# A hybrid decoder layer: the second half's attention projections take their token tiles from a pool that opens after the mixers

## The chip, the cores and the metric

One Trainium2 chip; the program runs on one of its cores. The metric is the device time of one execution in microseconds (us). TensorE is called PE, VectorE DVE, ScalarE ACT, GpSimd POOL and SyncE SP; PEld is PE's weight load. SP issues most of the DMAs, ACT issues some.

## What is computed

One decoder layer over 2048 tokens of width 1024. A combined projection feeds three groups of heads, whose outputs are joined and projected back; then a feed-forward part follows. The reference, cut to that:

```python
h = RMSNorm(x)
p = h @ w_in                      # columns split among three groups
A = mLSTM(p[...])                 # 4 heads, width 256, chunkwise
B = RWKV7(p[...])                 # 4 heads, width 256, delta-rule state
C = diff_attention(p[...])        # 4 heads, width 512, causal, blocks of 128 queries
x = x + concat(A, B, C) @ w_out
x = x + relu(RMSNorm(x) @ w_ff_up)**2 @ w_ff_down
return RMSNorm(x)
```

All of it is float32 in and out. The kernel multiplies in a split form: each operand is a high and a low part, and a product is three matmuls (`mm3`, L182 to L184: high by high, high by low, low by high).

## The kernel before

**Halves and columns.** The tokens stand as four column blocks of 512, two to a half. `Proj` holds the normalised tokens of one half as 16 tiles of 128x512 in a high and a low part (`hhi`, `hlo`). `start(half)` makes them: for each of the 16 tiles it loads 256 KB (`raw`, a tile `xk` from the pool `xp`, three buffers), multiplies it by the norm's factors on DVE (L324), writes the high part on ACT (L174) and the low part on DVE or POOL by turns (L175). Since `hhi` and `hlo` have one buffer for each column block, a second `start` overwrites them.

**Projections.** `feat` keeps weights stationary and runs 24 matmuls of 512 columns into one of two PSUM buffers `pd`; `token` keeps tokens stationary and runs 24 matmuls of 256 columns. `cols_a` makes the attention's columns of one half: four `feat` units (keys into `akh`, `akl`, queries into `aqh`, `aql`) of four `pd` tiles each, 384 matmuls of 512, and two `token` units (values into `av`) of eight tiles each, 384 matmuls of 256. All results go to DRAM.

**Mixers.** Sixteen iterations of `Rwkv` (prepare, scores, invert, chain, post: L505 to L777) and of `Mlstm` (up to L939) work on 128 tokens each, software-pipelined over five iterations: when iteration 15 is prepared, 12 is in its chain. The chain is a recurrence over the state `rST` with two steps to an iteration. Each step goes from PE (L717, L720) to a DVE copy `rZ`, to PE (L725), to copies `rUE` and `rUO`, to PE (L730, L733), and to DVE again (L735, L740). `post` ends with four POOL operations, transposes on PE (L772), copies on ACT (L774) and stores to `mixT` (L777).

**Order.** A scheduler places the instructions of each engine in one list, ahead of time, by priorities: the mixers have numbers from 100000 on, the projections 1000000, so that projections stand as filler between the mixers' operations wherever their data and buffers allow it. Pools are opened and closed like a stack, from a left and from a right side; a tile that takes the space of a closed pool waits for the last users of that space. The mixers' pools `rp` and `mp` lie on the right and close with `mctx.close()`; the pools of `Attention` (L942) open in that space, so its work can't begin before the mixers' end either. `Attention.run(c)` works on one column block: scores (L1004, L1005), their eviction with a maximum (L1008), exponentials (L1016), transposes (L1029), copies `PT` (L1031) and products with the values (L1034). `attn.run(0)` and `attn.run(1)` need only the first half's columns, `attn.run(2)` and `attn.run(3)` need both. Then comes `Tail`: four column blocks, each with an out-projection from `mixT`, a norm and the feed-forward matmuls. It is filler behind the attention.

In the built list of before the second half's projections stand among the last mixer iterations; the values' last part stands beside the first attention block.

Of the kernel before, what the change touches and what calls it, by code (L numbers as in the profile page):

```python
# [10 lines left out]
F32 = mybir.dt.float32  # L11
# [9 lines left out]
P = 128  # L21
# [4 lines left out]
T = 512  # L26
# [14 lines left out]
def load(nc, i, out, in_):  # L41
    (nc.sync if i % 2 == 0 else nc.scalar).dma_start(out, in_)
# [6 lines left out]
class Lane:  # L49


    def __init__(s, tc, p):
        s.tc, s.p = tc, p
# [94 lines left out]
def norm(tc, e, sp, raw, pp, ptag, src, gofs, emit, w=T):  # L148

    nc = tc.nc  # L150
    n = w // P
    acc = sp.tile([P, T], F32, name="nacc", tag="nacc", bufs=1)[:, :w]
    for k in range(KT):
        if k == 0:
            nc.scalar.activation(acc, src[k], AF.Square)
        else:
            sq = raw()[:, :w]
            nc.scalar.activation(sq, src[k], AF.Square)
            nc.vector.tensor_tensor(acc, acc, sq, ALU.add)
    ps = pp.tile([P, T], F32, name="nps", tag=ptag)  # L160
    for tt in range(n):
        nc.tensor.matmul(ps[:, tt:tt + 1], acc[:, tt * P:(tt + 1) * P], e.ones[:, 0:1], start=True, stop=True)
    sm = sp.tile([P, 3, 4], F32, name="nsm", tag="nsm", bufs=2)[:, :, :n]
    nc.vector.tensor_scalar(sm[:, 0], ps[:, 0:n], 1.0 / D, NORM_EPS, ALU.mult, ALU.add)
    rsqrt(nc, e, sm[:, 1], sm[:, 0], sm[:, 2])
    ps = pp.tile([P, T], F32, name="nps", tag=ptag)[:, :w]
    bcast_rows(nc, e, raw()[:, :w], ps, sm[:, 1])
    nc.scalar.copy(acc, ps)
    for k in range(KT):
        emit(k, src[k], e.vf[:, gofs + k:gofs + k + 1], acc)  # L170
# [48 lines left out]
class Proj:  # L219


    def __init__(s, ctx, tc, e, xt, pools):
        s.tc, s.e, s.xt = tc, e, xt
        s.hhi, s.hlo, s.rst, s.rcol = {}, {}, {}, {}
        s.last = e.cp.tile([P, 5], F32, name="last")
        tc.nc.gpsimd.memset(s.last, 0.0)

        s.qlast = e.cp.tile([P, 4, 3], F32, name="qlast")
        tc.nc.gpsimd.memset(s.qlast, 0.0)
        s.ep = ctx.enter_context(tc.tile_pool(name="ep", bufs=2))  # L230
        s.evp = (s.ep, 3)
        s.hp = ctx.enter_context(tc.tile_pool(name="hp", bufs=1))
        s.w = Weights(tc, e, ctx.enter_context(tc.tile_pool(name="wp1", bufs=2)), 5, 528)
        s.xp = ctx.enter_context(tc.tile_pool(name="xp", bufs=2))
        s.pd = ctx.enter_context(tc.tile_pool(name="pd", bufs=2, space=PSUM))

        d, a, m, i, c, l = (s.pd, "pd"), *[(pools[k], k) for k in ("pa", "pm", "pi", "pc", "pl")]
        s.pn, s.more = (l, i), ((d, d, m, m), (a, c, d, d))

    def raw(s, half, c, k):  # L240
        x = s.xp.tile([P, T], F32, name="xk", tag="xk", bufs=3)
        load(s.tc.nc, k, x, s.xt[half * 2 + c, k])
        return x

# [937 lines left out]
def tile_hybrid_layer(ctx: ExitStack, tc: tile.TileContext, xt, wi, wg, wm, wo, wu, wd, vf, vg, lw, hb, tb, lq, cm, out, dbg=None, upto=9):  # L1182
# [23 lines left out]
    e.state = State(tc, keep)  # L1206
    NG = HALF // RC
    mctx = ExitStack()
    lctx, actx = ExitStack(), ExitStack()
    with tc.using_default_side("right"):  # L1210
        pa = mctx.enter_context(tc.tile_pool(name="pa", bufs=1, space=PSUM))
        pm = mctx.enter_context(tc.tile_pool(name="pm", bufs=2, space=PSUM))
# [3 lines left out]
    pr = Proj(lctx, tc, e, xt, dict(pa=pa, pm=pm, pi=pi, pc=pc, pl=pl))  # L1216
# [46 lines left out]
    mctx.close()  # L1263
    with tc.using_default_side("right"):
        attn = Attention(actx, tc, e)
    for c in range(2):
        attn.run(c)
    pr.start(1)
    pr.cols_a(wi)
    lctx.close()  # L1270
    for c in range(2, 4):
        attn.run(c)
# [105 lines left out]
```

## Time and profile before

| | us |
|---|---|
| median of 3 runs | 3096.33 (3092.64 to 3100.31) |
| the profiled execution | 3105.86 |
| its span, from the first to the last instruction | 3104.0 |
| PE busy | 2976.4 |
| DVE busy | 1759.6 |
| ACT busy | 1219.4 |
| POOL busy | 1108.4 |

Times in the trace count from the span's start. A matmul's end is modelled, so that consecutive matmuls overlap in the rows; their pace is the distance of their starts. The granted clock is a share of the full 2.4 GHz; half of it is the other level, so a mean between 0.5 and 1 in a window says which part of it ran at 1.2 GHz.

### The profile page before, as it was taken

The page shows a single profiled execution, that of the slowest core. Times are in us where ns is not written, and L with a number is a line of the kernel's source. Part 1 is how long each engine was busy: PE and PEld are TensorE (multiplying, and loading weights), DVE is VectorE, ACT ScalarE, POOL GpSimd, SP SyncE. Part 2 cuts the span into 40 slices and gives each one's busy share as a digit, 9 for nine tenths or more (in the row PEclk, how much of TensorE's full clock was granted, in tenths as well). Part 3 has the DMA queues.
Part 4 walks back from the last instruction along what each step waited for, and adds up shares of the span by engine and source line. Part 5 has one row for each costly group of instructions (what it writes and reads, how often), then busy time and mean ns, then how long its engine had stood idle before and what let it go on. Part 6 is the DMA issues. An engine that isn't in the chain of part 4 may idle for free.

```text
span 3104.0 us, 47480 instructions
## 1 busy us (share of the span) xinstructions
PE 2976.4 (96%) x17232; PEld 2447.8 (79%) x17232; DVE 1759.6 (57%) x4087; ACT 1219.4 (39%) x2421; POOL 1108.4 (36%) x1063
## 2 busy tenths in 40 slices
PE   8999999899989979999999999999999999999997
PEld 6887877777867867888888878888787888888885
DVE  6486788967884356556455665554365333333335
ACT  5342333423332445454545454444344222222223
POOL 4443344534443213433334433433454222222213
PEclk9999999999999979999999999999999999999998
DMA  5434332544343553444445444342442211111111
GB/s 177 142 108 122 85 93 67 149 118 117 91 122 111 164 144 109 117 123 110 108 110 152 111 132 103 91 120 75 128 143 79 69 51 52 41 48 50 52 42 65
DMA packets 284484, 317.38 MB, mean 102 GB/s; under 512 B 99253, under 2 KB 160982, under 8 KB 284250
## 3 DMA queue, kind: packets, MB, share of 16 engines
q1 hardware_dynamic: 203050, 213.02, 24.4%
q10 hardware_dynamic: 81200, 101.34, 11.3%
q8 instruction: 136, 2.23, 0.3%
q14 instruction: 98, 0.80, 0.1%
HBM read 256.82 MB, written 57.43 MB: 101 GB/s over the span
## 4 chain that ended last, share of the span: by engine, by line
PE 67%; DVE 7%; DMA 4%; ACT 1%; issue 1%; POOL 1%; SPq 0%; ACTq 0%; DVEq 0%; POOLq 0%
PE pd L182 11%; PE pd L184 11%; PE pd L183 11%; PE py L182 7%; PE py L183 7%; PE py L184 7%; PE pO L1034 4%; PE pS L1004 2%; PE pS L1005 2%; PE pT L1029 2%; DMA Qd<-aql 1%; PE pi L677 1%; DMA traw<-mixT 0%; DVE E L1008 0%; DVE E L1023 0%
## 5 line engine op out<-in xcount | busy, mean ns | idle before, releaser
L175 POOL TENSOR_TENSOR wlo<-wraw,whi 128x512 fp32r<-128x512 f32 (+2 forms) x560 | 763.1, 1375 | 1293.4 <-ACT whi L174 796.6
L174 ACT ACTIVATE whi<-wraw 128x512 fp32r<-128x512 f32 (+2 forms) x560 | 347.4, 626 | 676.6 <-PE py L183 392.8
L1154 DVE TENSOR_TENSOR x<-py,x 128x512 f32<-128x512 f32 x512 | 350.7, 689 | 458.6 <-PE py L184 456.2
L182 PE MATMUL pd<-hh,whi 128*128 128x512 f32 x1280 | 503.2, 396 | 9.3 <-ACT hh L174 9.2
L183 PE MATMUL pd<-hl,whi 128*128 128x512 f32 x1280 | 504.4, 395 | 0.4 <-DVE hl L175 0.4
L184 PE MATMUL pd<-hh,wlo 128*128 128x512 f32 x1280 | 501.9, 395 | 0.0
L182 PE MATMUL py<-ah,whi 128*128 128x512 f32 x1024 | 404.8, 398 | 1.5 <-ACT whi L174 1.3
L183 PE MATMUL py<-al,whi 128*128 128x512 f32 x1024 | 400.8, 394 | 0.6 <-DVE al L175 0.6
L184 PE MATMUL py<-ah,wlo 128*128 128x512 f32 x1024 | 399.4, 394 | 0.2 <-POOL wlo L175 0.2
L182 PEld LDWEIGHTS pd<-hh,whi 128*128 128x128 f32 x1280 | 241.0, 189 | 62.0 <-ACT hh L174 10.5
L183 PEld LDWEIGHTS pd<-hl,whi 128*128 128x128 f32 x1280 | 241.8, 189 | 53.2 <-DVE hl L175 1.1
L184 PEld LDWEIGHTS pd<-hh,wlo 128*128 128x128 f32 x1280 | 241.9, 189 | 52.1 <-issue 0.2
L1008 DVE TENSOR_SCALAR_CACHE_REDUCE E<-pS 128x512 f32<-128x512 f32 (+4 forms) x320 | 185.4, 606 | 128.3 <-PE pS L1005 86.0
L175 DVE TENSOR_TENSOR al<-traw,ah 128x512 fp32r<-128x512 f32 x128 | 112.2, 878 | 222.8 <-ACT ah L174 222.2
L182 PE MATMUL pd<-hhi,whi 128*128 128x512 f32 x544 | 225.1, 416 | 10.8 <-ACT hhi L279 8.0
L182 PEld LDWEIGHTS py<-ah,whi 128*128 128x128 f32 x1024 | 192.6, 188 | 44.6 <-ACT whi L174 1.7
L184 PEld LDWEIGHTS py<-ah,wlo 128*128 128x128 f32 x1024 | 192.5, 188 | 43.7 <-POOL wlo L175 0.6
L183 PEld LDWEIGHTS py<-al,whi 128*128 128x128 f32 x1024 | 192.7, 188 | 42.5 <-DVE al L175 0.8
L183 PE MATMUL pd<-hlo,whi 128*128 128x512 f32 x544 | 224.1, 414 | 0.0
L184 PE MATMUL pd<-hhi,wlo 128*128 128x512 f32 x544 | 223.5, 413 | 0.4 <-POOL wlo L175 0.4
L182 PE MATMUL pd<-whi,hhi 128*128 128x256 f32 (+1 forms) x640 | 190.0, 297 | 4.8 <-ACT ev L352 2.8
L183 PE MATMUL pd<-wlo,hhi 128*128 128x256 f32 (+1 forms) x640 | 190.3, 297 | 0.0
(367 smaller groups left out, 5189.6 us busy)
## 6 DMA issues: line engine op xcount, KB each, us to landing
wraw<-in_wu ACTq DMA_DIRECT2D x96, 256.0 KB, 3.1
wraw<-in_wu SPq DMA_DIRECT2D x96, 256.0 KB, 3.1
wraw<-in_wd ACTq DMA_DIRECT2D x96, 256.0 KB, 3.0
wraw<-in_wd SPq DMA_DIRECT2D x96, 256.0 KB, 3.0
wraw<-in_wi ACTq DMA_DIRECT2D x48, 256.0 KB, 3.3
wraw<-in_wi SPq DMA_DIRECT2D x48, 256.0 KB, 3.3
xk<-in_xt ACTq DMA_DIRECT2D x32, 256.0 KB, 3.7
xk<-in_xt SPq DMA_DIRECT2D x32, 256.0 KB, 3.2
```

The lines of the kernel that those rows point to most:

```text
L174: nc.scalar.activation(hi, src, AF.Copy)
L175: lo_eng.tensor_tensor(lo, src, hi.bitcast(F32), ALU.subtract)
L182: nc.tensor.matmul(out, sh, mh, start=(i == 0), stop=False)
L183: nc.tensor.matmul(out, sh, ml, start=False, stop=False)
L184: nc.tensor.matmul(out, sl, mh, start=False, stop=(i == n - 1))
L677: PE.matmul(q[HS[h2], pcx * 64:(pcx + 1) * 64], lhsT[pcx][h2], rhs[pcx][h2], start=True, stop=True)
L1004: PE.matmul(s_[:, :k1 - k0], Q[c][0][:, qs], Kst[c][:, k0:k1], start=True, stop=False)
L1005: PE.matmul(s_[:, :k1 - k0], Q[c][1][:, qs], Kst[c][:, k0:k1], start=False, stop=not last)
L1008: V.tensor_scalar(E[:, k0:k0 + w], s_[:, :w], 0.125, None, ALU.mult, ALU.max, accum_out=mb[:, j:j + 1])
L1029: PE.transpose(t_[:, b * P:(b + 1) * P], Es[0][:, j * T + b * P:j * T + (b + 1) * P], e.ident)
L1034: PE.matmul(o[:, 0:P], pt[:, b * P:(b + 1) * P], vt[:, kb], start=(kb == 0), stop=(kb == i))
L1154: nc.vector.tensor_tensor(x2[d], ps, x2[d], ALU.add)
```

## The change

The second call of `start(1)`, the one for the attention's columns, no longer takes its `xk` tiles from `xp`. A new pool `xq` is opened on the right side, behind the pools of `Attention`, after the mixers' pools are closed, and `raw` uses it when it is there. It has one tag with three buffers, as before. The pool is closed after the projections, ahead of `lctx`. No instruction is added or removed; the lists are built anew with the other dependency.

```diff
         s.evp = (s.ep, 3)
+        s.rp = None
...
     def raw(s, half, c, k):
-        x = s.xp.tile([P, T], F32, name="xk", tag="xk", bufs=3)
+        x = (s.rp or s.xp).tile([P, T], F32, name="xk", tag="xk", bufs=3)
         load(s.tc.nc, k, x, s.xt[half * 2 + c, k])
         return x
...
-    lctx, actx = ExitStack(), ExitStack()
+    lctx, actx, qctx = ExitStack(), ExitStack(), ExitStack()
...
     mctx.close()
     with tc.using_default_side("right"):
         attn = Attention(actx, tc, e)
+
+        pr.rp = qctx.enter_context(tc.tile_pool(name="xq", bufs=1))
     for c in range(2):
         attn.run(c)
     pr.start(1)
     pr.cols_a(wi)
+    qctx.close()
     lctx.close()
     for c in range(2, 4):
         attn.run(c)
```

In the new file every line from L232 on has a number that is one higher, so L677 is L678 there and L1004 is L1005.

On PE, among the last mixer iterations (`XE`, `XO`, `rBK`: the scores' operands; `rW`, `rVbd`, `rTbd`: those of the inversion), a piece of the list before is this:

```order
L182 MATMUL pd<-hhi,whi 128x512
L183 MATMUL pd<-hlo,whi 128x512
L184 MATMUL pd<-hhi,wlo 128x512
L612 MATMUL pm<-XE_730,rBK 128x192
L612 MATMUL pm<-XO_731,rBK 128x192
L677 MATMUL pi<-rVbd,rW 64x64 x8
```

After, the same scores stand so:

```order
L897 MATMUL pa<-mC,mcv 128x65
L678 MATMUL pi<-rTbd,rMB 64x64 x8
L678 MATMUL pi<-rVbd,rW 64x64 x8
L613 MATMUL pm<-XE_730,rBK 128x192 x2
L613 MATMUL pm<-XO_731,rBK 128x192 x2
L726 MATMUL pc<-rZ,rV_9195 64x64 x4
```

The second half's projections (L182 to L184 on `hhi`, `whi`, 512 columns wide) have left this stretch. Up to the last mixer matmul there is no projection in it any more: the first half's last one stands 15 rows ahead of this piece, and 145 more rows of mixers follow.

The end of the mixers on PE, after (`rMB`: the chain's last product; `rY`: the transposes of the last post):

```order
L734 MATMUL pc<-rUE,rMB 64x64
L734 MATMUL pc<-rUO,rMB 64x64
L773 MATMUL pm<-ident,rY 64x128 x4
L182 MATMUL pd<-hhi,whi 128x512 x2
L183 MATMUL pd<-hlo,whi 128x512
L184 MATMUL pd<-hhi,wlo 128x512
```

Behind the last transposes the second half's first projection matmuls stand, and the first matmuls of attention begin 13 rows later. In the list before, all 384 matmuls of 512 columns stand ahead of these transposes.

On SP, the loads and stores around the mixers' end, before (`av`: the second half's values; `ag`, `Kst`: the attention's constants and keys):

```order
L777 DMA mixT_173<-ryT 64x2x128 x2
L355 DMA av_169<-ev 128x256
L953 DMA ag<-in_tb 128x512
L970 DMA Kst<-akh_0_152 64x512
L971 DMA Kst<-akl_0_160 64x512
```

After:

```order
L42 DMA rVbd<-vd_126 64x4x64 x2
L940 DMA mixT_173<-myT 128x2x128
L778 DMA mixT_173<-ryT 64x2x128 x6
L42 DMA xk<-in_xt 128x512 x2
L954 DMA ag<-in_tb 128x512
L971 DMA Kst<-akh_0_152 64x512
L972 DMA Kst<-akl_0_160 64x512
L977 DMA Qd<-aqh_0_136 64x512
```

The loads of the second half's tokens (`xk`) have moved behind the mixers' last six stores and run into the attention's first loads. ACT issues the other half of them, likewise behind the last post's copies.

On PE, where attention ends (`osb`: its last transposes; `hh_23217` and on: the high parts of the third column block's out-projection, whose inputs include the attention's result), before, with buffer numbers:

```order
L184 MATMUL pd_23407<-hh_20951,wlo_23371 128x512
L1046 MATMUL pT_17310<-ident_63,osb_16913 128x128
L182 MATMUL pd_23407<-hh_20957,whi_23370 128x512
L183 MATMUL pd_23407<-hl_20958,whi_23370 128x512
L184 MATMUL pd_23407<-hh_20957,wlo_23371 128x512
L182 MATMUL py_23543<-ah_23130,whi_23520 128x512
L183 MATMUL py_23543<-al_23131,whi_23520 128x512
L182 MATMUL py_23551<-ah_23130,whi_23520 128x512
L183 MATMUL py_23551<-al_23131,whi_23520 128x512
L184 MATMUL py_23543<-ah_23130,wlo_23521 128x512
L184 MATMUL py_23551<-ah_23130,wlo_23521 128x512
L182 MATMUL pd_23463<-hh_23217,whi_23438 128x512
```

After, around the same out-projection's first matmul (`pd_23467<-hh_23221`):

```order
L184 MATMUL pd_23411<-hh_20955,wlo_23375 128x512
L182 MATMUL pd_23411<-hh_20961,whi_23374 128x512
L183 MATMUL pd_23411<-hl_20962,whi_23374 128x512
L184 MATMUL pd_23411<-hh_20961,wlo_23375 128x512
L182 MATMUL pd_23467<-hh_23221,whi_23442 128x512
L183 MATMUL pd_23467<-hl_23222,whi_23442 128x512
```

Before, the out-projection begins ten rows after the attention's last transpose (`pT`); after, the attention's last transpose stands 190 rows ahead of it, with feed-forward matmuls between them.

## Rows read from the trace of the kernel before

**Rows 1.** The page's first part: busy us, share of the span, instructions of PE.

```profile
PE 2976.4 (96%) x17232; PEld 2447.8 (79%) x17232; DVE 1759.6 (57%) x4087; ACT 1219.4 (39%) x2421; POOL 1108.4 (36%) x1063
```

**Rows 2.** Windows: busy us of PE, PEld, DVE, ACT, POOL; clock, DMA share, GB/s.

```profile
864.00:1000.00 136.00, 130.29 (x986) 101.47 (x984) 88.12 (x244) 38.79 (x90) 52.03 (x54) 0.95 0.38 115
1000.00:1030.00 30.00, 30.00 (x232) 27.68 (x229) 4.96 (x15) 8.14 (x19) 9.71 (x10) 1.00 0.36 108
1030.00:1066.00 36.00, 35.33 (x292) 33.77 (x290) 12.96 (x63) 14.65 (x47) 4.96 (x4) 1.00 0.58 165
1066.00:1160.00 94.00, 72.35 (x319) 53.86 (x317) 57.30 (x214) 45.35 (x126) 16.60 (x13) 0.78 0.56 153
1160.00:1240.00 80.00, 75.22 (x387) 61.61 (x386) 50.97 (x124) 41.07 (x86) 29.52 (x22) 0.96 0.42 115
```

**Rows 3.** Groups of PE in 864 to 1030: projection matmuls of the second half.

```profile
L182 PE MATMUL pd<-hhi,whi 128*128 128x512 f32 x128 | 53.1, 415 | 0.0
L184 PE MATMUL pd<-whi,hlo 128*128 128x256 f32 x55 | 15.6, 284 | 0.0
```

**Rows 4.** Timeline of PE, start and length in us: projection and mixer matmuls.

```profile
863.99 0.39 PE L182 MATMUL pd<-hhi,whi 128*128 128x512 f32 x1
...
1000.61 0.40 PE L182 MATMUL pd<-hhi,whi 128*128 128x512 f32 x1
1000.84 0.39 PE L183 MATMUL pd<-hlo,whi 128*128 128x512 f32 x1
...
1005.10 0.45 PE L725 MATMUL pc<-rZ,rV 64*64 64x64 f32 x8
...
1010.21 0.27 PE L730 MATMUL pc<-rUE,rTE 128*64 128x64 f32 x1
```

**Rows 5.** Groups of DVE in 864 to 1030 that are not the mixers'.

```profile
L370 DVE TENSOR_TENSOR evl<-pd,evh 128x512 fp32r<-128x512 f32 x16 | 11.0, 686 | 22.5 <-ACT evh L369 22.5
L324 DVE SCALAR_TENSOR_TENSOR xk<-xk,vf,nrst 128x512 f32<-128x512 f32 x7 | 5.9, 867 | 0.0
...
L175 DVE TENSOR_TENSOR hlo<-xk,hhi 128x512 fp32r<-128x512 f32 x4 | 3.2, 802 | 1.3 <-ACT hhi L174 1.3
```

**Rows 6.** Windows, columns as in rows 2: the densest DVE stretch, one feature pass.

```profile
500.00:600.00 100.00, 91.35 (x832) 74.14 (x830) 94.27 (x240) 40.86 (x97) 49.87 (x58) 1.00 0.37 104
573.00:617.00 44.00, 36.30 (x261) 29.54 (x259) 42.94 (x97) 20.11 (x47) 21.12 (x19) 0.92 0.65 180
```

**Rows 7.** Timeline of DVE: the last iterations of the Rwkv chain and its post.

```profile
982.77 0.42 DVE L690 TENSOR_TENSOR rV<-pi,rVbd 128x256 f32<-128x256 f32 x1 [3.24 <-PE pi L677]
...
1000.16 0.29 DVE L722 COPY rZ<-pc 128x128 f32<-128x128 f32 x1 [1.64 <-PE pc L720]
...
1005.60 0.28 DVE L726 COPY rUE<-pc 64x128 f32<-64x128 f32 x1 [0.64 <-PE pc L725]
...
1016.97 0.42 DVE L754 TENSOR_TENSOR rY<-rY,rst 128x256 f32<-128x256 f32 x1
```

**Rows 8.** Timelines of POOL and SP: end of the last iteration's post.

```profile
1019.91 0.74 POOL L760 TENSOR_TENSOR rY<-rY,rgt 128x256 f32<-128x256 f32 x1
...
1024.84 1.23 SPq L777 DMA_DIRECT2D mixT<-ryT  x2
```

**Rows 9.** The page's sixth part: loads of token tiles, median us to landing.

```profile
xk<-in_xt SPq DMA_DIRECT2D x32, 256.0 KB, 3.2
```

**Rows 10.** Waits of PE in 1066 to 1160: us in total, times, longest.

```profile
PE pO L1034 <- ACT PT L1031: 4.2, 6, 2.0
```

**Rows 11.** Windows, columns as in rows 2: around the end of attention.

```profile
2180.00:2200.00 20.00, 13.77 (x65) 10.52 (x63) 6.34 (x14) 7.82 (x15) 8.65 (x7) 0.99 0.40 126
2200.00:2220.00 20.00, 18.48 (x70) 14.81 (x71) 8.50 (x14) 7.77 (x13) 5.53 (x5) 0.84 0.49 139
```

**Rows 12.** Timeline of PE: first matmul of the third out-projection.

```profile
2201.52 1.22 PE L182 MATMUL pd<-hh,whi 128*128 128x512 f32 x2 [6.29 <-ACT hh L174]
```

## The prediction

> **What bounds the kernel now.** First the busy table: PE is busy for 2976.4 of 3104.0 us, 96%, no other engine for more than 57% [rows 1]. Both kernels issue the same instructions, so a change of order can only win where PE idles or runs at its lower clock, and it loses where it makes new time of that kind. So I read the windows around the moved work, 864 to 1240 us [rows 2], and reckon in each how much of it PE lost: its length less its busy time multiplied by the granted clock (0.5 would be 1.2 GHz throughout, 1 is 2.4 GHz).
>
> The second half's first projection matmul starts at 863.99 [rows 4]. From there to 1000, 136 - 130.29 x 0.95 = 12.2 us are lost; to 1030 nothing; to 1066, 0.7; to 1160, 94 - 72.35 x 0.78 = 37.6; to 1240, 80 - 75.22 x 0.96 = 7.8. The sum is 58.3 us. The reader is to see where: while the last mixer iterations run, PE is full, because the second half's projections fill the gaps. The loss follows when these are used up: attention alone waits for its own copies and evictions, 4.2 us for `PT` alone [rows 10], and half of its time the clock is low. One more loss lies at the end of attention: from 2180 to 2220 it is 40 - 13.77 x 0.99 - 18.48 x 0.84 = 10.8 us [rows 11], of which 6.29 are one wait, PE for `hh` of the third out-projection [rows 12].
>
> **What the change does.** It takes the filler from the first stretch, where it is worth most, and puts it into the second. Both ends have to be priced.
>
> *The mixers bare.* Up to about 864 us the lists are alike, so the mixers stand there where they stand before. How much PE work have they left? Before, 864 to 1030 holds 384 matmuls of 512 columns (128 on each of three lines) and 164 of 256 [rows 3]. The first start 0.23 us apart (1000.61, 1000.84) [rows 4]; for the others I take half of it, 0.115, an estimate by their columns. That is 88.3 + 18.9 = 107.2 us. Of 166 us 58.8 remain; less the 12.2 lost, 46 us are mixer work. PE will thus have 46 us of work until the mixers end, and what matters is how long they take alone.
>
> Two ways to it. By DVE: it is busy for 88.12 + 4.96 = 93.1 us in 864 to 1030 [rows 2], of which 11.0 + 5.9 + 3.2 = 20.1 are the projections' [rows 5]; 73.0 us are the mixers'. At the densest that this trace shows, 94.27% [rows 6], they take 77 us. The last part is a chain and can't be as dense: from the last `rV` at 982.77 to the last `rY` at 1016.97 there are 34.2 us [rows 7]. It holds two steps of the recurrence. In one, the matmul on `rZ` starts at 1005.10 although `rZ` is there at 1000.45, and that on `rUE` at 1010.21 although `rUE` is there at 1005.88: 4.65 + 4.33 = 9.0 us behind queued projections [rows 4, 7]. Without them the chain takes 34.2 - 18 = 16.2 us, some 5 of which are DVE's and in the 77 already (an estimate from the 0.28 and 0.42 us of such rows). Behind the last `rY` come POOL's four operations, transposes, copies and the stores, 9 us from 1016.97 to the last store's end at 1026.07 [rows 7, 8]; then the first `xk` lands after 3.2 us [rows 9], and its multiplication and split take 1.5 (0.75 us each, from rows 5): 13.7. The sum is 77 + 11.2 + 13.7 = 102 us. By the chain: from 863.99 to 1017.39 there are 153.4 us now; the three iterations left have six steps, each relieved of 9.0 us of filler: 99.4, and 13.7 behind it makes 113. I take the middle, 107 us, and keep 95 (the first way, if half of the stores' and loads' time is hidden) and 128 (the second, with 15 us for the slow clock, below). The first projection matmul then starts at 971, and 107 - 46 = 61 us are lost, 49 more than before.
>
> *The feature pass.* Sixteen tiles must be loaded and split before PE has all its filler. Before, this lay beside full PE work; a pass takes 44 us with DVE busy for 42.94 of them [rows 6]. Beside attention, where DVE has 57.30 us of work in 94 [rows 2], I take 40. Two PSUM buffers get three matmuls each from a tile: 6 x 0.23 x 16 = 22 us. Attention does 56.4 us of full-speed work in 94 alone [rows 2]; at half that rate beside the projections it adds 12. So 6 us are lost, and 2 for the clock to come back: 8, with 2 and 14 as ends.
>
> *Attention with filler.* Behind that, the rest of the 107 us of projections stands among the first two attention blocks, and the 37.6 us lost there go. Some of it comes back at the change to the out-projections: of the 7.8 us of 1160 to 1240 I leave 5, with 0 and 12 as ends. So the stretch loses 61 + 8 + 5 = 74 where it lost 58.3: +15.7.
>
> *The end of attention.* Attention now starts beside the projections, ahead of most of them, and so it also ends earlier among the feed-forward matmuls: its last transposes stand 190 rows ahead of the third out-projection. At 0.23 us [rows 4] these are some 44 us, which cover the 6.29 us wait and the rest of the 10.8 us. I take -9, with 0 and -10.8 as ends.
>
> The sum is +15.7 - 9 = +6.7 us against the profiled execution's 3105.86, thus 3112.6. That execution lies 9.5 us above the median of the runs, 3096.33, which I take as the level of what is to be measured: **3103**. A measurement of this kernel can tell about 0.3%, 9.3 us, from no change, so the forecast is within 0.3%, near its slower edge. In other words: slower if the second half's first projection matmul starts after about 974 us, with all else as above, faster if it starts before 955.
>
> **The rivals.**
>
> *Slower: the bare stage runs at 1.2 GHz.* In the stretch with attention alone, PE busy for 77% in rows of short matmuls, the granted clock fell to 0.78 [rows 2], so PE was at 1.2 GHz for nearly half of it; with the mixers alone it will be busy for 46 of 107 us, 43%. At half speed the 46 us become 92, still less than the stage, so PE is not its bound; but its matmuls lie on the chain PE, DVE, PE. If a third of the added 46 us falls on the chain (PE shares it with DVE's copies and with the transfers), the stage is 15 us longer: +22, 3118. It decides from 3 us of such lengthening. For it speaks the fall of the clock at far more load; against it that my second way, 113 us, may hold spare waits already.
> The Trainium skill, "TensorE: Matmul & The Clock Gate", section "HAM oscillation — how this bites in real kernels", says that a PE that keeps waiting between bursts has its clock cut again and starts each next burst slow. It speaks against this change; the 0.78 of rows 2 agrees with it, and by it the time would be this rival's 3118 instead of the forecast's 3103.
>
> *Faster: the mixers are DVE's alone.* If the stage is done after 95 us, the pass loses only 2 because attention fills it, and the change to the out-projections 2, the stretch loses 49 + 2 + 2 = 53, 5 less than before; with the end of attention at -9 this is -14, 3082. For it speaks that the 73.0 us of DVE contain rows slowed by POOL's and the projections' traffic, such as 867 ns for the `xk` multiplication [rows 5]; against it that DVE is busy for 93.1 of 166 us now, 56%, so that latencies, not work, may set the pace.
>
> *It doesn't hold anything back.* The lists show the loads of `xk` behind the mixers' last stores on SP and on ACT, so this can't hold for most of them. It would give 3096.
>
> **How the numbers follow.** Forecast 0.41, the slow clock 0.35, the bare DVE 0.20, nothing held back 0.04. The forecast's own range, with the stage at 95 at its lower end and with the stage at 113 and the pass at 14 at its upper, is 3091 to 3115: most of it lies within 0.3%, and what spills over the slower edge is about what the slow clock's lower part gives back. Faster by over 0.3%: 0.21; within 0.3%: 0.41; slower: 0.38. The range for 8 in 10 takes in most of both rivals: low 3084, just short of the faster one's time; high 3124, the slow clock with the pass at its upper end.
>
> **What would show it.** In the profile after: the first matmul on `hhi` of the second half at 971 (955 to 985); from 864 to there PE busy below half and DVE above 70%; no projection between. The granted clock in that stretch: near 0.9 for the forecast, below 0.7 for the slow clock. The pass of L325 over 40 us, with PE busy for 80% of it. From there to the out-projection a PE that is full and at full clock, in place of the 0.78. At the end of attention no wait of 6.29 us. The prediction is wrong in its main term if the bare stage is shorter than 95 us or longer than 128, wrong in its second if attention with projections still waits for `PT` as now, and wrong in its third if the third out-projection waits elsewhere.

## The result, and the profile after

| | before | after |
|---|---|---|
| median, us | 3098.32 (4 runs, 3092.64 to 3101.84) | 3121.77 (4 runs, 3120.91 to 3129.20) |
| profiled execution, us | 3105.86 | 3122.12 |
| its span, us | 3104.0 | 3120.4 |

The change makes the kernel slower: the ratio is 1.0083 (95% interval 1.0060 to 1.0105), +23.4 us between the medians. The forecast was +6.7. A second measurement, shown below, gives 1.0089 (1.0051 to 1.0128).

The windows of the kernel after answer [rows 2] and [rows 11]; the columns are as there, PE's busy time first, the granted clock third from the end:

```profile
864.00:1000.00 136.00, 96.40 (x720) 76.08 (x719) 88.55 (x274) 31.83 (x87) 43.06 (x51) 0.61 0.29 80
1000.00:1030.00 30.00, 28.02 (x142) 22.10 (x141) 17.20 (x53) 11.31 (x32) 5.42 (x5) 1.00 0.65 194
1030.00:1066.00 36.00, 35.25 (x179) 28.57 (x178) 15.38 (x57) 15.10 (x41) 9.57 (x8) 1.00 0.55 161
1066.00:1160.00 94.00, 93.76 (x672) 85.56 (x671) 46.62 (x162) 41.26 (x110) 13.67 (x11) 1.00 0.50 147
1160.00:1240.00 80.00, 71.76 (x373) 58.30 (x371) 41.78 (x114) 38.80 (x79) 31.73 (x23) 0.96 0.58 162
1240.00:1260.00 20.00, 17.88 (x82) 13.86 (x82) 14.32 (x35) 10.10 (x23) 7.89 (x7) 0.83 0.35 91
2180.00:2200.00 20.00, 17.89 (x78) 14.19 (x77) 10.48 (x15) 11.02 (x19) 8.19 (x7) 1.00 0.59 180
2200.00:2220.00 20.00, 20.00 (x90) 16.45 (x89) 4.46 (x8) 7.94 (x14) 9.79 (x9) 1.00 0.36 98
```

Three things have turned over. The stretch from 864 to 1000, full before, is at a clock of 0.61, and PE is busy for 71% of it. Attention from 1066 to 1160, which lost 37.6 us before, loses 94 - 93.76 = 0.2. And the end of attention, 10.8 us before, loses 2.1. What is new lies behind 1160: 80 - 71.76 x 0.96 = 11.1 us, and 20 - 17.88 x 0.83 = 5.2 in the next 20.

The bare stretch in the timelines of the kernel after, PE (first the first half's last projection matmul, last the second half's first), then DVE (the last `rV` and the last `rY`, as in [rows 7]), then SP:

```profile
860.19 0.28 PE L184 MATMUL pd<-whi,hlo 128*128 128x256 f32 x1
...
958.54 1.06 PE L773 MATMUL pm<-ident,rY 128*64 128x128 f32 x4 [8.81 <-POOL rY L761]
970.19 1.22 PE L182 MATMUL pd<-hhi,whi 128*128 128x512 f32 x2 [10.58 <-ACT hhi L174]
```

```profile
940.33 0.42 DVE L691 TENSOR_TENSOR rV<-pi,rVbd 128x256 f32<-128x256 f32 x1 [1.22 <-PE pi L678]
...
954.80 0.42 DVE L755 TENSOR_TENSOR rY<-rY,rst 128x256 f32<-128x256 f32 x1
```

```profile
940.59 22.49 SPq L778 DMA_DIRECT2D mixT<-ryT  x6
964.90 0.84 SPq L42 DMA_DIRECT2D xk<-in_xt  x2
```

From 860.19 to 955.22 the mixers take 95.0 us alone, and 15.0 more go by until the first projection matmul: 110.0 us in all, where the forecast had 107. The last chain, 34.6 us before from `rV` to the end of `rY`, takes 14.9.

### The profile page after: what moved, and what is told of

The parts are those of the page before. It is cut to its first block, busy times and chain, and to the rows that moved or that the text cites. A ratio compares the mean times of both kernels' runs of the same rounds, so it can differ in the third digit from the quotient of the medians.

```text
span 3120.4 us, 47517 instructions
## 1 busy us (share of the span) xinstructions
PE 2977.2 (95%) x17232; PEld 2454.5 (79%) x17232; DVE 1763.1 (57%) x4087; ACT 1215.7 (39%) x2421; POOL 1117.2 (36%) x1063
## 4 chain that ended last, share of the span: by engine, by line
PE 69%; DVE 7%; DMA 4%; ACT 1%; POOL 1%; issue 1%; SPq 0%; ACTq 0%; DVEq 0%; POOLq 0%
PE pd L184 11%; PE pd L182 11%; PE pd L183 11%; PE py L182 7%; PE py L183 7%; PE py L184 7%; PE pO L1035 4%; PE pS L1005 2%; PE pS L1006 2%; PE pT L1030 2%; DMA traw<-mixT 1%; DMA xk<-in_xt 1%; PE pi L678 0%; DVE xk L325 0%; PE pm L613 0%
## 5 line engine op out<-in xcount | busy, mean ns | idle before, releaser
L175 POOL TENSOR_TENSOR wlo<-wraw,whi 128x512 fp32r<-128x512 f32 (+2 forms) x560 | 772.6, 1393 | 1240.7 <-ACT whi L174 793.7
L182 PE MATMUL pd<-hh,whi 128*128 128x512 f32 x1280 | 503.9, 396 | 5.4 <-ACT hh L174 4.9
L184 PE MATMUL pd<-hh,wlo 128*128 128x512 f32 x1280 | 500.2, 394 | 0.0
L182 PE MATMUL py<-ah,whi 128*128 128x512 f32 x1024 | 403.5, 397 | 1.8 <-DVE x L1155 1.8
L184 PE MATMUL py<-ah,wlo 128*128 128x512 f32 x1024 | 398.8, 393 | 0.0
L182 PEld LDWEIGHTS pd<-hh,whi 128*128 128x128 f32 x1280 | 241.0, 189 | 59.3 <-ACT hh L174 6.5
L184 PEld LDWEIGHTS pd<-hh,wlo 128*128 128x128 f32 x1280 | 241.3, 189 | 51.8 <-issue 0.2
L182 PE MATMUL pd<-hhi,whi 128*128 128x512 f32 x544 | 225.2, 420 | 20.3 <-ACT hhi L174 11.1
L182 PEld LDWEIGHTS py<-ah,whi 128*128 128x128 f32 x1024 | 192.4, 188 | 44.9 <-DVE x L1155 2.2
L184 PE MATMUL pd<-hhi,wlo 128*128 128x512 f32 x544 | 226.5, 419 | 0.7 <-POOL wlo L175 0.7
L184 PEld LDWEIGHTS py<-ah,wlo 128*128 128x128 f32 x1024 | 192.3, 188 | 43.5
L182 PE MATMUL pd<-whi,hhi 128*128 128x256 f32 (+1 forms) x640 | 187.5, 293 | 2.3 <-ACT ev L353 1.4
```

The source lines that it names most:

```text
L175: lo_eng.tensor_tensor(lo, src, hi.bitcast(F32), ALU.subtract)
L182: nc.tensor.matmul(out, sh, mh, start=(i == 0), stop=False)
L184: nc.tensor.matmul(out, sl, mh, start=False, stop=(i == n - 1))
```

## The experiments

Each ratio is to runs of the kernel before that stood beside it on the same chip; its median there was 3092.81 in the first group, 3092.51 in the second, 3101.31 in the third and 3098.78 for the last run. A stretch's loss is reckoned as in the prediction, from windows of 20 us.

### How much may be held back

The first question was whether the loss is in proportion to what is held back, or comes only when too little is left beside the mixers. Three kernels hold back less: not the token tiles, but the tiles `ev` into which results are evicted come from the late pool, from a chosen unit on. A fourth keeps the change for one of the two column blocks.

```diff
 # e1: values; e2: second unit of queries and values; e3: queries and values
+            if s.late and u == 0:        # e2: u == 1
+                s.evp = s.late
             s.feat(wi[6 + u], ...)       # e1: at the value units
...
+        pr.late = (qctx.enter_context(tc.tile_pool(name="xq", bufs=1)), 3)
 # e4, on the kernel after:
-        x = (s.rp or s.xp).tile(...)
+        x = (s.rp if s.rp and c else s.xp).tile(...)
```

> Only the values of the second half are held back: the tiles into which they are evicted come from the pool that opens after the mixers; token tiles, keys and queries are as in the kernel before. In the PE list 62 matmuls of 256 columns (7 us at 0.117 us) move from ahead of the mixers' end to behind it. Theory A, account by stages: projections can leave the mixers' stage at no cost as long as the mixers' own 46 us of PE work and what is kept (384 x 0.23 + 48 x 0.117 = 94 us) fill more than the 107 us that the mixers take alone; what is held fills the attention's gaps one for one. That gives 0 to -7 us, about 3094. Theory B, every us of projections moved behind the mixers costs in proportion to what the whole change cost (+23.4 us for 101 us moved, 0.23 per us): +2 us, 3100.

> The same pool for the evictions from the second unit of queries on: that unit and all values are held back, keys and the first unit of queries stay among the mixers. Moved behind the mixers' end: 48 matmuls of 512 and 110 of 256 columns, 24 us. Theory A: kept are 336 x 0.23 + 46 = 123 us, more than 107, so the mixers' stage loses no more than before, and attention's loss of 54 us falls by up to 24: -15 to -24 us, about 3079. Theory B: +5 us, 3104.

> The same from the first unit of queries on: all queries and values held back, only the keys stay among the mixers. Moved: 144 matmuls of 512 and 110 of 256 columns, 46 us. Theory A: kept are 240 x 0.23 + 46 = 101 us, just under the 107 us of the mixers alone, so that stage begins to lose (5 to 15 us more than before), while attention's loss falls by up to 43: -25 to -10 us, about 3080. Theory B: +11 us, 3109.

> The change, but only the tiles of the second of the half's two column blocks come from the new pool; the first block's eight tiles are loaded and split among the mixers as before. In the PE list 48 matmuls of 512 columns (11 us) go back among the mixers, and half of the feature pass is done ahead. Theory A: the mixers' stage loses 11 us less and the pass behind it, 13 us of loss after the change, about 7 less: 15 to 18 us below the change's 3121.8, about 3105. Theory B: 0.23 x 11 = 2.5 us below it, 3119.

Measured: e1 3088.08 us, ratio 0.9993 (0.9978 to 1.0008); e2 3088.66, 0.9993 (0.9975 to 1.0011); e3 3088.59, 0.9986 (0.9967 to 1.0005); e4 3107.07, 1.0054 (1.0039 to 1.0069). Theory B, a price in proportion, falls by e2, e3 and e4: up to 46 us held back cost nothing that the medians show. (For e1 alone its +2 us lies inside the interval.) But A is wrong as well for e2 and e3, which should have won 15 us and more, and 10 us and more; only e1 and e4 came as it said. The windows tell why. These are PE's from 960 to 1000 in e3 and in e4:

```profile
960.00:1000.00 40.00, 22.77 (x124) 17.79 (x121) 10.07 (x35) 8.47 (x22) 9.62 (x10) 0.70 0.40 120
```

```profile
960.00:1000.00 40.00, 25.72 (x108) 19.08 (x108) 19.89 (x50) 13.63 (x34) 12.42 (x8) 0.79 0.62 194
```

e3 loses 40 - 22.77 x 0.70 = 24 us there. The projections that it keeps are used up early, the last of them at 953.92 with the next at 981.23, while the last `rY` ends at 970.4. So the end of the mixers stays bare although 55 us were kept: the last chain, the post, its stores, the first loads. A's condition looked at the sum of work and not at where in the stage it lies.

The second thing that these runs show is what a kept projection costs. The length of the mixers' stage, from the start of the first half's last projection matmul to the end of the last `rY`, against the projections of the second half that ran in it (matmuls of 512 columns at 0.23 us, of 256 at 0.117):

| | kept, us | stage starts | last `rY` ends | stage, us |
|---|---|---|---|---|
| after | 0 | 860.2 | 955.2 | 95.0 |
| e4 | 11.0 | 861.7 | 955.6 | 93.9 |
| e3 | 55.2 | 849.2 | 970.4 | 121.2 |
| e2 | 77.3 | 853.1 | 994.7 | 141.6 |
| e1 | 93.9 | 860.0 | 1013.4 | 153.4 |
| before | 95.2 | 863.9 | 1017.4 | 153.5 |

The starts lie up to 15 us apart, ahead of the edited place, so the ends alone would mislead. The 11 us of e4 cost nothing; 55 us make the stage 26 us longer, and from there on each further microsecond adds 0.8 us (32.3 us for 40.0). The projections that looked free in the kernel before, on a PE that was full, delayed the mixers by 58 us. That fits what the whole change costs, some 20 us and not 95.

### One execution or the kernel, one chip or the change

Both kernels were run once more. The edit is none.

> The kernel before once more, for a second profile of it. Its first profiled execution, 3105.86 us, lay above all the unprofiled ones. Theory R: some of the time that PE lost there belongs to that one execution; then the second profile, at a usual time near 3093, shows some 10 us less loss, in single windows. Theory K: the losses are the kernel's, and the second profile shows each window's loss within 2 us: 24 us from 840 to 1060, 43 from 1060 to 1160, 11 from 1160 to 1300, 11 at the end of attention.

> The changed kernel once more, against the kernel before on one chip and with a second profile. If the loss is the order's, the ratio is again 1.006 to 1.010 (some 3116 where the kernel before takes 3093), and the profile shows the mixers' last DVE operation 95 us after the first half's last projection matmul and the second half's first one 15 us behind it. If a part of the 23 us was the one chip's or the one execution's, the ratio falls to 1.002 to 1.005.

e5: 3106.61 us in its one execution, profiled. Two windows of it, to be laid beside those of [rows 2]:

```profile
1066.00:1160.00 94.00, 72.28 (x330) 53.73 (x329) 58.07 (x221) 45.96 (x130) 17.40 (x14) 0.80 0.57 156
1160.00:1240.00 80.00, 75.18 (x389) 61.62 (x387) 51.01 (x124) 40.99 (x84) 29.54 (x22) 0.96 0.42 115
```

They agree with the first profile within 2 us, as theory K has it. By windows of 20 us the four stretches that it names lose 15.2, 37.0, 7.9 and 10.8 us in the first profile and 14.6, 35.9, 7.9 and 10.4 in e5; the 24, 43 and 11 us that the expectation gives for the first three are not found. So the losses from which the sum was made are no accident. Something else stays open: both profiled executions of the kernel before are 8 to 14 us longer than the medians of its other runs (single ones of these reach 3114.94), while e1 to e4 and the changed kernel's first profile lie within 5 us of theirs, and e9's lies 10 us below. No run here shows where the unprofiled executions of the kernel before are faster.

e6: 3122.53 us, ratio 1.0089 (1.0051 to 1.0128). Its last `rY` ends 96.0 us after the first half's last projection matmul, and the second half's first one starts 15.1 us behind it, as expected. The slowdown belongs to the change.

The four traces also show how much of it lies behind the edited place. The first half's last projection matmul starts at 863.88 and 864.65 in the two profiles of the kernel before, and at 860.19 and 856.56 in those of the changed kernel. From there to the end of the span it is 2240.1 and 2240.2 us before, 2260.2 and 2258.6 after: the change costs 18.5 to 20.1 us there. Why the kernels differ ahead of that place no run here shows.

### Does the slow clock lengthen the mixers?

The rival that I gave 0.35 was that the bare mixers run at 1.2 GHz and take longer by it. The clock did fall, to 0.56 in the mean from 860 to 955. To keep it up, PE got small matmuls that nothing reads, as filler in place of the projections.

```diff
     pr.start(0)
     pr.cols_a(wi)
+    for g in range(40):                  # e8: 14
+        ps = pr.pd.tile([P, T], F32, name="pd", tag="pd")
+        for j in range(30):
+            nc.tensor.matmul(ps[:, 0:P], e.idr, e.mk, start=(j == 0), stop=(j == 29))
     mctx.close()
```

> The change, with 1200 small matmuls (128x128, constants, into the projections' PSUM buffers, not read by anything) as filler behind the first half's projections, which is more work than the kernel has: its time is to be read with that in mind. They stand among the last mixer operations up to their end. The mixers' stage is measured from the first half's last projection matmul to the mixers' last DVE operation: 95 us after the change, with the granted clock at 0.5 for most of it. Theory C, the slow clock lengthens the mixers' chain: with PE kept at full clock the stage is 10 us or more shorter, 85 or less. Theory Q, what lengthens the stage is what stands ahead of the mixers in PE's queue: it is no shorter, and longer by most of what the small matmuls take, 120 to 150 us.

> The same with 420 of the small matmuls, which end ahead of the last two iterations' chains. Theory C: as long as they last the clock stays at full speed, and the stage is 3 to 8 us shorter than 95. Theory Q: the few small ones fit into gaps; the stage is 95 to 105 us. With the 48 matmuls of 512 columns of the run with the second block alone, 11 us of filler, it was 93.9.

The same stretch, from the first half's last projection to the last `rY`, in the kernel after, in e8 and in e7, one window each:

```profile
860.00:955.00 95.00, 71.90 (x659) 58.98 (x657) 69.23 (x234) 19.47 (x58) 31.02 (x40) 0.56 0.16 38
```

```profile
872.00:976.00 104.00, 84.66 (x1074) 70.93 (x1071) 69.89 (x233) 19.14 (x57) 31.26 (x40) 0.78 0.15 34
```

```profile
852.00:967.00 115.00, 111.96 (x1570) 98.27 (x1569) 69.97 (x234) 19.46 (x58) 31.28 (x40) 0.88 0.14 32
```

With the clock at 0.78 the stretch is 104 us long and with 0.88 115, against 95 at 0.56. Theory C's forecasts, 85 or less and 87 to 92, fail; Q's came for e8 and were too long for e7. But the small matmuls stand in the queue as well, so these two runs can't say what the clock alone costs. The times of the two, one execution each (3129.78 and 3140.88), start from stages that lie 19.5 us apart before the edited place (852.2 and 871.7) and are not compared.

Single chain steps can say it. A step has three waits of DVE for PE: for `rUE`, for `rsn` and for the next `rZ`. Here they are first in e3, where no filler stands among them and the granted clock is 1.00 (954 to 961.5), then in the last chain of the kernel after, where it is 0.50 (944 to 951):

```profile
958.61 0.28 DVE L729 COPY rUE<-pc 64x128 f32<-64x128 f32 x1 [0.55 <-PE pc L728]
960.19 0.29 DVE L738 TENSOR_TENSOR rsn<-pc,rST 128x128 f32<-128x128 f32 x1 [1.29 <-PE pc L736]
...
961.91 0.29 DVE L725 COPY rZ<-pc 128x128 f32<-128x128 f32 x1 [0.46 <-PE pc L723]
```

```profile
946.70 0.29 DVE L723 COPY rZ<-pc 128x128 f32<-128x128 f32 x1 [0.90 <-PE pc L721]
947.78 0.28 DVE L727 COPY rUE<-pc 64x128 f32<-64x128 f32 x1 [0.79 <-PE pc L726]
949.85 0.29 DVE L736 TENSOR_TENSOR rsn<-pc,rST 128x128 f32<-128x128 f32 x1 [1.78 <-PE pc L734]
```

They sum to 2.30 us at the high clock and 3.47 at the low one (e9 has the same 0.55, 1.29 and 0.46 at a clock of 1.00, 967.5 to 973.8): a bare step is 1.2 us longer at 1.2 GHz. So the slow clock does lengthen the chain, by some 7 us over the six steps of the last three iterations if all of them lie on the path (an estimate from these rows). In e7 the same three waits of the last step are 1.75, 2.55 and 1.77 us at a clock of 1.00: there the small matmuls in the queue cost more than the clock gives back. What the clock costs outside the chain, as from 870 to 920, where PE of the kernel after is busy for 47.1 of 50 us at 0.50, stays open.

### Where the held projections should come free

If the hole is the end of the mixers, the held projections should start when the last chain is done, and not when the mixers' space is released. Four kernels do that by another means: the evictions of the held units multiply by a column of ones that POOL derives from the state `rST` after a chosen chain. Token tiles are those of the old pool, so the feature pass lies among the mixers.

```diff
+        s.gate, s.held = e.cp.tile([P, 1], F32, name="gate"), False
...
-                sc = 1.0 if s.known else s.rcol[c][:, tt % 4:tt % 4 + 1]
+                sc = s.gate if s.held else 1.0 if s.known else s.rcol[c][:, tt % 4:tt % 4 + 1]
...
-            nc.scalar.activation(h_, ps, AF.Copy)
+            nc.scalar.activation(h_, ps, AF.Copy, scale=s.gate if s.held else 1.0)
...
+            s.held = half == 1 and u >= 1     # in cols_a; e9: from the queries on, e11: u >= 0
             s.feat(wi[8 + u], ...)
...
                 rw.chain(xs[it - 3])
+                if it - 3 == 15:              # e12: 14
+                    nc.gpsimd.tensor_scalar(pr.gate, e.state.rST[:, 0, 0:1], 0.0, 1.0, ALU.mult, ALU.add)
```

> Queries and values are held back as in the run with both held by the pool, but by another means: their evictions multiply by a column of ones that POOL makes from the Rwkv state after the last iteration's chain, so they come free when the chain ends, ahead of the last post, its stores and the release of the mixers' space; token tiles come from the old pool. Theory D: of the 20 us that PE lost between 960 and 1000 in that run, 12 to 16 lay behind the chain's end (post, stores, the attention's loads) and are filled now: about 3075. Theory E: projections next to the mixers displace them whenever they come, so the time stays within 3 us of that run's 3088.6.

> The same gate, from the second unit of keys on: only the first unit of keys (96 matmuls of 512 columns) and two more PSUM tiles, 33 us in all, stay among the last mixers. Theory D: up to 95 - 46 = 49 us of projections fit beside the mixers without making them longer (11 us didn't, 55 us made them 26 us longer), so the mixers end about 97 us after the first half's last projection, their end is covered, and 100 us of projections are left for the attention: loss to 1300 us about 53 where the run with queries and values held by the pool had 70; about 3072. The hole at the change to the out-projections comes back, some 20 us, since the projections end after the first attention block. Theory E: what is won at the mixers is lost at that change: 3085 to 3092.

> The same gate for all of the second half's attention columns: as much is held back as in the run with the second block alone (48 matmuls of 512 columns stay ahead), but the feature pass is done among the mixers and the projections come free at the chain's end, not when the space is released. Against that run (3107.1) it tells what the place and the time of the release cost by themselves. Theory D: the mixers' stage keeps its 38 us of loss, the 20 us between the last chain and the first full matmuls and the rest of the pass go: about 3085. Theory E: no release helps that comes behind the mixers' chain: 3100 to 3107.

> The same as the run with the gate from the second unit of keys on, but the column of ones is made after the chain of the last iteration but one. In the PE list 190 of the held matmuls of 512 columns more (44 us) then stand ahead of the mixers' end. Theory D: what stands beside the last chain displaces it nearly one for one once the gaps are full; the mixers end some 30 us later and the attention's gaps keep 40 us less to fill them: 3085 to 3095, some 10 to 15 us more than that run. Theory F: an earlier release is as good or better, since PE is idle during the last chain: 3070 to 3077.

Measured: e9 3078.99 us, ratio 0.9930 (0.9909 to 0.9951); e10 3076.53, 0.9915 (0.9899 to 0.9931); e11 3083.85, 0.9937 (0.9917 to 0.9956); e12 3087.46, 0.9964 (0.9946 to 0.9981). All four are faster than both kernels, e10 by 0.85% of the kernel before. PE from 960 to 1000 in e9, which is to be laid beside e3's, and in e11, beside e4's:

```profile
960.00:1000.00 40.00, 34.38 (x270) 27.49 (x267) 13.18 (x41) 10.65 (x25) 14.68 (x18) 0.87 0.29 87
```

```profile
960.00:1000.00 40.00, 40.00 (x184) 32.30 (x184) 10.67 (x37) 13.30 (x30) 13.38 (x12) 1.00 0.72 215
```

e9 loses 10 us where e3 lost 24, and e11 nothing where e4 lost 20, with as much work held back. So theory D holds: it was not the holding back that cost, but that the release hung on the mixers' space, which comes free only behind the last post's stores, and that the pass over the token tiles hung on it too. One part of D failed: with 35 us kept in e10 the stage was to be as short as bare, about 97 us, and it is 114.2 (the feature pass stands in it too), so filler isn't free just because the sum of work leaves room. Against e11, e10 has 35 us of projections ahead of the mixers' end in place of 13, and the mixers end 9 us later (969.6 against 960.7); the intervals of the two ratios overlap. e12 shows the other side: released one chain earlier, 78 us run ahead of the mixers' end instead of 35, this comes at 1004.2 instead of 969.6, and the ratio is 0.9964, clear of e10's.

## Why the prediction was wrong

The direction of the sum and the time's place in the range were right, but the forecast, no measurable change, was not: +23.4 us where the sum had +6.7. The step that failed is the change to the out-projections; the shift to the level of the medians was off as well. By the prediction's steps:

**The bare mixers: nearly right in length, wrong in the clock.** 107 us were forecast until the first projection matmul, 110.0 were measured; less the 46 us of work, 64 us are lost instead of 61. The two ways had 102 and 113. That a chain step gives back the 9.0 us that it spent behind projections was right: the last chain, forecast at 16.2 us from the start of `rV` to the start of `rY`, took 14.5. But two signs failed: PE was to be busy below half of the stage at a clock near 0.9, and it was busy for 76% at 0.56. The 107 us hold no price for that clock, so the near fit may be two errors that cancel; no run separates them.

**The slow clock: it came, its price did so in part at most.** The rival's mark, a clock below 0.7, is there, and the 15 us of added length aren't: the stage is 3 us longer than forecast. The Trainium skill's rule on the clock ("TensorE: Matmul & The Clock Gate", "HAM oscillation — how this bites in real kernels") agrees with this trace as to the clock, 0.56 in the bare stretch. As to the time, the rows of e3 and of the kernel after give 1.2 us for a chain step, some 7 for six, and what the clock costs beside the chain is open. The measured 3121.77 lies near this rival's 3118, but not by the stage that the rival lengthened.

**The feature pass: small.** These windows of the kernel after lie around it:

```profile
960.00:980.00 20.00, 9.24 (x29) 6.85 (x30) 8.06 (x10) 4.42 (x8) 4.48 (x3) 0.58 0.57 172
980.00:1000.00 20.00, 16.54 (x75) 11.63 (x74) 15.04 (x42) 9.86 (x25) 8.27 (x7) 1.00 0.74 218
1000.00:1020.00 20.00, 18.02 (x96) 14.02 (x95) 14.38 (x44) 9.52 (x28) 5.42 (x5) 1.00 0.83 236
```

Of the first, 10.2 us belong to the bare stage (it ends at 970.19); 20 - 9.24 x 0.58 - 10.2 = 4.4 remain, then 3.5 and 2.0: 10 us, forecast 8. The 16 multiplications take 36 us from the first start to the last end where 40 were taken. The 2 us "for the clock to come back" had no row behind them; in this trace the clock is 0.50 from 970 to 975 and 0.84 from 975 to 980, some 3 us lost. And the 0.75 us for a multiplication and a split aren't what [rows 5] shows, 0.87 and 0.80; that is 0.2 us.

**The change to the out-projections: the step that failed.** Of the 7.8 us lost from 1160 to 1240 I left 5, with 12 as the upper end. It is 11.1 there and 17.8 up to 1300 (16.4 in e6), where the kernel before loses 7.9 up to 1300. The 7.8 us were the wrong loss to start from. In the kernel before the out-projections begin at 1072.1; most of what it loses behind 1160 lies around the first matmul of the norm that follows them (`nps`), at 1199.31. After, that matmul comes at 1242.19. The 20 us around it, before and after:

```profile
1189.30:1209.30 20.00, 17.73 (x83) 14.16 (x82) 13.79 (x36) 9.21 (x20) 6.86 (x5) 0.83 0.24 68
```

```profile
1232.20:1252.20 20.00, 17.93 (x83) 13.63 (x81) 12.28 (x29) 9.62 (x20) 7.30 (x6) 0.83 0.22 66
```

They lose 5.3 and 5.1 us (5.3 and 4.6 in e5 and e6): the norm's loss is not less for the change, it only comes 43 us later. The change to the out-projections itself comes on top of it. This is PE in the kernel after, behind the last projection matmul at 1166.00:

```profile
1166.00 0.28 PE L184 MATMUL pd<-whi,hlo 128*128 128x256 f32 x1
...
1168.95 1.11 PE L1047 MATMUL pT<-ident,osb 128*128 128x128 f32 x4 [1.79 <-DVE osb L1044]
1173.55 1.22 PE L182 MATMUL pd<-hh,whi 128*128 128x512 f32 x2 [3.48 <-ACT hh L174]
```

and the load that it needs, SP and then the ACT split of what was loaded:

```profile
1166.34 0.33 SPq L42 DMA_DIRECT2D wraw<-in_wo  x1
```

```profile
1171.31 1.67 ACT L174 ACTIVATE whi<-wraw 128x512 fp32r<-128x512 f32 x3 [3.91 <-DMA wraw<-in_wo]
1172.88 1.66 ACT L174 ACTIVATE hh<-traw 128x512 fp32r<-128x512 f32 x3
```

The out-projection's pools open in the space of the projections, so its first weights can't be loaded until the last projection is done (SP waits at this load for PE's `pd`, L184): issue at 1166.34, first matmul at 1173.55, although the first attention block, whose result it needs, was stored at 1127.59. In the kernel before the same hole exists, but there the projections end at 1065.5 and the first out-projection matmul comes at 1072.1, in the stretch of attention alone. Attention's own matmuls fill most of it: PE waits for 1.6 us in it, after for 5.3. The 10 us behind the last projection, before and after:

```profile
1065.80:1075.80 10.00, 8.39 (x37) 5.64 (x36) 7.75 (x20) 6.05 (x15) 4.68 (x3) 0.83 0.59 183
```

```profile
1166.30:1176.30 10.00, 4.32 (x14) 2.46 (x14) 5.44 (x12) 4.79 (x10) 4.87 (x4) 0.74 0.57 154
```

They lose 3.0 and 6.8 us, and from 1160 to 1180 it is 8.1 after (8.4 in e6). I had booked the 37.6 us of that stretch as attention's and let all of it go. So a part of the 37.6 was not won but moved, and grew: the hole now stands where little else is there to fill it. In e1 to e4 and e9 to e12 the out-projections begin at 1082 to 1155, so what those kernels lose from 1160 to 1300 (3.8 us in e12 to 12.1 in e4) doesn't contain this hole and neither supports nor contradicts the account. A kernel with the out-projection's first operands in space of their own would test it; that was not tried. The cause is thus read from the traces of before, e5, after and e6, and not shown by an experiment.

**The end of attention: right.** 10.8 - 2.1 = 8.7 us are won, forecast 9, and the wait of 6.29 us [rows 12] is gone; the longest that is left there is 1.8.

**The level: off by some 7 us.** The sum was added to the profiled execution, and 9.5 us were then taken off, since that execution lay so far above the median of its runs. The changed kernel's profiled execution lies 0.35 above its own. Between the two profiled executions the difference is 16.3 us, between the medians 23.4; the 7 us between the two stand in no term of the sum, and no run places them.

**The sum.** 3 us too little for the bare stage, 2 for the pass, 13 for the change to the out-projections and the norm: +6.7 becomes some +25. That this lies next to the +23.4 of the medians is luck. The traces from which it is made have only 18.5 to 20.1 us behind the edited place, so this way of adding up losses comes out 4 to 7 us too high here.

## What to carry to other kernels

Filler in an engine's list isn't free because the engine was idle: look how far the end of the work beside it moves, counted from a place that both kernels share (here 58 us for 95 us of filler), before pricing what its removal costs or gives. A hole that lies inside another hole has no price until the other is filled; when a stall is to be filled, list every wait inside it that will then stand alone. And what is held back should be released by the event that matters, here the last chain, not by the release of memory: here the first held matmul came 15 us behind the last post's DVE work, and with it PE lost 20 us more from 960 to 1000 (e4 against e11).

## What was not expected of the hardware

PE's busy time says little of a chain. In the bare stretch its rows show 71.90 of 95 us busy at a clock of 0.56, for what was reckoned as 46 us of work at full speed; a reader would take it for three quarters full. Yet e7's small matmuls, 65.1 us busy in the row below (852 to 968), went into the same stretch and made it only 20 us longer, with the clock at 0.88:

```profile
L1267 PE MATMUL pd<-amk,aidr 128*128 128x128 bf16 x929 | 65.1, 227 | 0.0
```
